# Two products of an up projection change places in a written order of work

## The chip, the cores and the metric

The kernel runs on one core of one Trainium2 chip. What counts is the time on the device, in microseconds (us), as the median of several executions. The engines are named as in the profile: PE is TensorE (its matmuls; PEld its weight loads), DVE is VectorE, ACT is ScalarE, POOL is GpSimd, and SP is SyncE, which here only issues DMAs. Each engine has a queue of its own and works through it in order; an instruction that has to wait for another engine holds up all that stands behind it on its own.

## The reference

One layer of a hybrid decoder on 1024 tokens with 1024 features, in float32:

```
h = x + W_o [ RMSNorm(attention(u)) ; RMSNorm(ShortConv(u)) ],   u = RMSNorm(x) @ W_in
a = rms_norm(h) @ w_up;  gate, up = split(a)            # 2 x 2816 features
gate = causal_dwconv(gate, ffn_conv_w) + ffn_conv_b     # three taps along the tokens
h = h + (silu(gate) * up) @ w_down
h = h + sigmoid(rms_norm(h) @ w_pg) * (p @ w_pe)
```

The change lies in the second line, the up projection, at its very beginning.

## The kernel before

Float32 products are made of halves: a number is split in a high half, rounded to the form that PE takes (`fp32r`), and a low half, the rest. A product of two such numbers is three matmuls (high by high, high by low, low by high). ACT casts the high half, and DVE subtracts it from the number to get the low half.

**The up projection.** The 2816 features are 22 blocks `f` of 128. For a block, gate and up by two halves of the tokens by two halves of the 1024 inputs make a 2 by 2 block product, which the kernel forms with seven products in place of eight (Strassen's scheme in Winograd's form). Product `(f, i)` is 12 matmuls of 128x512: four chunks `k` of the inputs by three halves. The table `PRODUCT` says for each `i` which combination of the activations it takes, in which PSUM accumulator it adds up, and which combination of the weights it takes:

```
    PRODUCT = {1: ("b11", "x", "a11"), 2: ("b21", "x", "a12"), 3: ("b22", "z", "s4"), 4: ("t4", "y", "a22"),
               5: ("t1", "z", "s1"), 6: ("t2", "y", "s2"), 7: ("t3", "y", "s3")}
```

So `(1, 2)`, the second product of block 1, takes the activations `b21` and the raw weights `a12` and adds onto `ux` of block 1, where `(1, 1)` has been. Behind `(f, 1)` stands a copy of `ux` to SBUF by ACT (tile `uv`, line 1084), and it has to be made before `(f, 2)` adds to the same accumulator. `(0, 5)` takes the activations `t1` (tiles `formt1` with the chunk's number) and the sum of weights `s1` = `a21` + `a22`, and it is the first to write `uz` of block 0; behind it DVE makes `uw` from `uz` and `uv` (line 1052), and only then may `(0, 3)` add onto `uz`.

**Weights.** `fetch` loads a raw quarter of a block's weights (tile `wup`, 256 KB, a DMA of SP's queue, line 91) and POOL adds or subtracts quarters to the sums (tile `wsum`, line 1010): for a block `s1`, `s2` = `s1` - `a11`, `s4`, `s3`. `split` then casts the high half on ACT (`wbh`, line 1023) and subtracts the low half on DVE (`wbl`, line 1024), four places of the order ahead of the product. `ahead` fetches, and thereby puts in the order of SP and POOL, seven to nine places ahead.

**Activations.** In the same written order, ahead of and between the first products, stand four pairs `("A", k)`: the output projection of rows `k` and `k + 4` for the second half of the tokens (PSUM tiles `bp`), and in between eight small products `("E", m)` (tiles `be`, copied by ACT to `emb` and stored to `eD`). A pair is followed by a chain: DVE scales `bp` (line 882) and adds the residual to get `hm` (line 884), ACT multiplies by a gain to get `y` (line 890), DVE makes the combinations `yt` (line 904), ACT casts their high halves and DVE subtracts the low halves (both into `form`, lines 909 and 913). The chain of pair `k` gives chunk `k` of `t1`, `t2`, `t3`, `t4` and `b22`; the last chunk, `formt13` and its like, comes from `("A", 3)`.

**What sets the order.** All of this lies in a `manual_schedule`: the instructions stand on each engine as the loop over `order` emits them. Where tiles lie in SBUF is settled when the program is built (`auto_bufs=True`): tiles share places, and a tile that takes over a place waits for the last reader of the tile that was there.

Of the kernel before, what the change touches and what calls it, by code (L numbers as in the profile page):

```python
# [48 lines left out]
def _emit(nc, tc, d, out, tap=lambda *a: None):  # L49
# [909 lines left out]
    for m in range(KC):  # L959
# [4 lines left out]
        if m == 3:  # L964
# [23 lines left out]
           "s4": (OP.subtract, "a12", "s2")}  # L988
    AHEAD = 4
    order = [("A", 0), ("E", 0), ("E", 1), ("E", 2), ("A", 1), ("E", 3), ("E", 4), ("E", 5), ("A", 2), ("E", 6), ("E", 7),  # L990
             (0, 1), ("A", 3), (1, 1), (0, 2), (1, 2),
             (0, 5), (0, 6), (0, 3), (0, 7), (1, 5), (0, 4), (1, 6), (1, 3), (1, 7)]
    for f in range(2, NF):
        order += [(f, 1), (f - 1, 4), (f, 6), (f, 5), (f, 2), (f, 7), (f, 3)]
    order.append((NF - 1, 4))
# [364 lines left out]
def _build(arrays, tap=None):  # L1360
    nc = _bacc.Bacc("TRN2", target_bir_lowering=False, num_devices=1)
    d = {k: nc.dram_tensor("in_" + k, v.shape, _mybir.dt.from_np(v.dtype), kind="ExternalInput").ap()
         for k, v in arrays.items()}
    out = nc.dram_tensor("out_0", (KC, P, T), F32, kind="ExternalOutput").ap()
    with _tile.TileContext(nc, auto_bufs=True) as tc:  # L1365
        _emit(nc, tc, d, out, *([lambda n, a: tap(nc, n, a)] if tap else []))
    return nc
# [8 lines left out]
```

## Time and profile before

| | us |
|---|---|
| median of 3 executions | 1471.7 |
| lowest and highest of the 3 | 1469.31 and 1472.52 |
| the profiled execution, its own time | 1464.96 |
| its span, first to last instruction | 1463.1 |

The 1.9 us between span and own time lie around the instructions. Durations below come from the profiled execution, which was 6.7 us faster than the median of the timed ones; the profile's times count from the start of its span. The first block of the up projection begins at 667 us, and the whole projection ends at about 1113 us.

### The profile page before, as it was taken

The page shows a single profiled execution, that of the slowest core. Times are in us where ns is not written, and L with a number is a line of the kernel's source. Part 1 is how long each engine was busy: PE and PEld are TensorE (multiplying, and loading weights), DVE is VectorE, ACT ScalarE, POOL GpSimd, SP SyncE. Part 2 cuts the span into 40 slices and gives each one's busy share as a digit, 9 for nine tenths or more (in the row PEclk, how much of TensorE's full clock was granted, in tenths as well). Part 3 has the DMA queues.
Part 4 walks back from the last instruction along what each step waited for, and adds up shares of the span by engine and source line. Part 5 has one row for each costly group of instructions (what it writes and reads, how often), then busy time and mean ns, then how long its engine had stood idle before and what let it go on. Part 6 is the DMA issues. An engine that isn't in the chain of part 4 may idle for free.

```text
span 1463.1 us, 19683 instructions
## 1 busy us (share of the span) xinstructions
PE 1423.8 (97%) x7223; PEld 1161.9 (79%) x7223; DVE 990.0 (68%) x1612; ACT 605.1 (41%) x1240; POOL 477.5 (33%) x462
## 2 busy tenths in 40 slices
PE   7999999999999999998999999999999999999998
PEld 5787898997777777786788888888788887888787
DVE  7645467555788888788767887777786464377443
ACT  4110132136788898775423333333334322045311
POOL 3221242366445558202432334332330424002200
PEclk9999999999999999999999999999999999999999
DMA  7221214300000002274022212222216432241132
GB/s 263 75 73 45 88 39 150 133 1 1 1 1 1 1 1 87 75 260 148 29 86 87 69 61 87 87 87 86 86 52 219 160 139 88 75 169 44 53 99 80
DMA packets 52945, 123.91 MB, mean 85 GB/s; under 512 B 6001, under 2 KB 8945, under 8 KB 52849
## 3 DMA queue, kind: packets, MB, share of 16 engines
q1 hardware_dynamic: 52848, 122.65, 24.7%
q8 instruction: 57, 0.93, 0.3%
q14 instruction: 40, 0.32, 0.1%
HBM read 94.32 MB, written 28.31 MB: 84 GB/s over the span
## 4 chain that ended last, share of the span: by engine, by line
PE 50%; DVE 2%; issue 1%; ACT 0%; POOLq 0%; POOL 0%; ACTq 0%; DVEq 0%
PE uy L1044 12%; PE uz L1044 8%; PE ux L1044 8%; PE ba L103 6%; PE ba L102 6%; PE ba L101 6%; PE bd L103 1%; PE bd L102 1%; PE bd L101 1%; DVE wbl L1024 0%; DVE actl L1181 0%; DVE yt L904 0%; PE ba L165 0%; POOLq L1365 0%; DVE ua L1071 0%
## 5 line engine op out<-in xcount | busy, mean ns | idle before, releaser
L1044 PE MATMUL uy<-formt,wbh 128*128 128x512 f32 x528 | 165.2, 394 | 0.7 <-ACT wbh L1023 0.3
L694 POOL TENSOR_SCALAR P<-P,sc,consts 128x64 f32<-128x64 f32 (+8 forms) x192 | 130.4, 689 | 98.4 <-DVE sc L692 93.8
L1010 POOL TENSOR_TENSOR wsum<-wup,wup 128x512 f32<-128x512 f32 x44 | 74.8, 1700 | 266.4 <-DMA wup<-in_w_up 205.4
L677 DVE TENSOR_REDUCE nmax<-b 128x1 f32<-128x64 f32 (+8 forms) x192 | 96.9, 540 | 35.3 <-PE b L669 34.5
L1024 DVE TENSOR_TENSOR wbl<-wsum,wbh 128x512 fp32r<-128x512 f32 x88 | 77.1, 877 | 63.1 <-ACT wbh L1023 63.1
L1044 PEld LDWEIGHTS uy<-formt,wbh 128*128 128x128 f32 x528 | 99.0, 188 | 24.9 <-issue 1.2
L683 ACT ACTIVATE P<-b,nmax 128x64 f32<-128x64 f32 (+8 forms) x192 | 108.9, 576 | 18.9 <-DVE nmax L677 7.7
L1044 PE MATMUL ux<-formb,wbh 128*128 128x512 f32 x352 | 111.6, 398 | 5.1 <-ACT uv L1084 5.1
L102 PE MATMUL ba<-actl,wh 128*128 128x512 f32 x288 | 113.3, 394 | 1.9 <-DVE actl L1181 1.9
L103 PE MATMUL ba<-acth,wl 128*128 128x512 f32 x288 | 112.9, 393 | 0.0
L101 PE MATMUL ba<-acth,wh 128*128 128x512 f32 x288 | 112.1, 392 | 0.0
L143 DVE TENSOR_TENSOR wl<-wraw,wh 128x1024 fp32r<-128x1024 f32 (+3 forms) x85 | 89.2, 1052 | 23.2 <-POOL wh L142 10.8
L1044 PE MATMUL uy<-formt,wbl 128*128 128x512 f32 x264 | 104.4, 395 | 0.0
L719 PE MATMUL ba<-consts,P 128*128 128x128 f32 x592 | 90.2, 276 | 5.0 <-DVE pl L735 2.5
L1198 DVE TENSOR_TENSOR h<-h,ba 128x512 f32<-128x512 f32 x64 | 43.9, 686 | 71.8 <-PE ba L103 71.5
L142 POOL TENSOR_SCALAR wh<-wraw 128x1024 fp32r<-128x1024 f32 (+2 forms) x37 | 48.2, 1307 | 130.0 <-PE b L102 48.1
L719 PEld LDWEIGHTS ba<-consts,P 128*128 128x128 f32 x592 | 68.3, 142 | 23.7 <-issue 7.1
L1071 DVE SCALAR_TENSOR_TENSOR ua<-ug,consts,ua 128x1023 f32<-128x1023 f32 (+1 forms) x44 | 85.1, 1933 | 0.0
L735 DVE TENSOR_TENSOR pl<-ba,ph 128x512 fp32r<-128x512 f32 x120 | 78.8, 679 | 7.5 <-ACT ph L731 6.3
L1044 PEld LDWEIGHTS ux<-formb,wbh 128*128 128x128 f32 x352 | 67.0, 191 | 21.1 <-ACT uv L1084 5.5
L1100 ACT ACTIVATE ua<-ua 128x1024 f32<-128x1024 f32 x22 | 23.3, 1061 | 144.4 <-DVE ua L1071 144.4
L140 ACT CAST wh<-wraw 128x512 fp32r<-128x512 f32 (+2 forms) x48 | 30.3, 654 | 115.0 <-PE ba L102 102.5
(321 smaller groups left out, 3944.8 us busy)
## 6 DMA issues: line engine op xcount, KB each, us to landing
wup<-in_w_up SPq DMA_DIRECT2D x88, 256.0 KB, 4.1
aD<-ua SPq DMA_DIRECT2D x22, 512.0 KB, 2.9
t<-aD SPq DMA_DIRECT2D x22, 512.0 KB, 4.9
wraw<-in_w_down SPq DMA_DIRECT2D x32, 256.0 KB, 5.3
wraw<-in_wA SPq DMA_DIRECT2D x13, 512.0 KB, 3.6
hinc<-in_xT SPq DMA_DIRECT2D x16, 256.0 KB, 3.3
h<-t SPq DMA_DIRECT2D x16, 256.0 KB, 2.3
hin<-h SPq DMA_DIRECT2D x16, 256.0 KB, 4.5
```

The costliest lines, as they stand in the source:

```text
L101: pe.matmul(ps, ah, bh, start=first, stop=False)
L102: pe.matmul(ps, ah, bl, start=False, stop=False)
L103: pe.matmul(ps, al, bh, start=False, stop=last)
L143: dve.tensor_sub(lo, raw, f32(hi))
L677: dve.tensor_reduce(nmax[:, b:b + 1], ps[:, o:o + w], axis=AX.X, op=OP.max, negate=True)
L683: act.activation(pr[:, pc:pc + w], ps[:, o:o + w], AF.Exp, bias=nmax[:, b:b + 1], accum_out=den[:, b:b + 1])
L694: pool.tensor_scalar(pr[:, pc:pc + w], pr[:, pc:pc + w], sc[:, b:b + 1], gates[:, t, hd * 3 + b:hd * 3 + b + 1], op0=OP.mult, op1=OP.mult)
L719: pe.transpose(pt[0:k, r * P:(r + 1) * P], probs[u, r][:, pc:pc + k], ident)
L735: dve.tensor_sub(pl, pt[0:k], f32(ph))
L1024: dve.tensor_sub(lo, y, f32(hi))
L1044: pe.matmul(ps, a[:, k], b, start=new and k == n_mm == 0, stop=k == 3 and n_mm == 2, skip_group_check=not new)
L1071: dve.scalar_tensor_tensor(a[:, j:], y[:, 0:T - j], cw[:, 2 - j:3 - j], a[:, j:], op0=OP.mult, op1=OP.add)
```

## The change

`(0, 5)` stood right behind `(1, 2)` and now stands right ahead of it:

```diff
     order = [("A", 0), ("E", 0), ("E", 1), ("E", 2), ("A", 1), ("E", 3), ("E", 4), ("E", 5), ("A", 2), ("E", 6), ("E", 7),
-             (0, 1), ("A", 3), (1, 1), (0, 2), (1, 2),
-             (0, 5), (0, 6), (0, 3), (0, 7), (1, 5), (0, 4), (1, 6), (1, 3), (1, 7)]
+             (0, 1), ("A", 3), (1, 1), (0, 2), (0, 5), (1, 2),
+             (0, 6), (0, 3), (0, 7), (1, 5), (0, 4), (1, 6), (1, 3), (1, 7)]
```

Everything that hangs on a place of the order moves along: the 12 matmuls, the two splits, the loads and sums, and what follows a product (`uw` behind `(0, 5)`, the gate `ug` behind `(1, 2)`). The build also lays 664 tiles at other places in SBUF, so that some waits are other ones.

On PE, after the products `(0, 1)`, `("A", 3)`, `(1, 1)`, before the change (the first row is the end of `(0, 2)`; `ux_1669` belongs to block 1, `wbh_1647` are the weights `a12` of block 1, `wbh_1667` those of `s1` of block 0; in brackets what a row waits for):

```order
L1044 MATMUL ux_1642_7556<-formb213_1524_7088,wbl_1641_7553 128x512
L1044 MATMUL ux_1669_7654<-formb210_1503_7001,wbh_1647_7576 128x512 [waits Activation_49]
L1044 MATMUL ux_1669_7654<-formb210_1503_7001,wbh_1647_7576 128x512
L1044 MATMUL ux_1669_7654<-formb210_1503_7001,wbl_1648_7577 128x512 [waits DVE_49]
L1044 MATMUL ux_1669_7654<-formb211_1509_7028,wbh_1647_7576 128x512 x2
```

And in the changed kernel (`wbh_1647` now holds `s1` of block 0, `wbh_1667` now `a12` of block 1):

```order
L1044 MATMUL ux_1642_7556<-formb213_1524_7088,wbl_1641_7553 128x512
L1044 MATMUL uz_1680_7702<-formt10_1554_7208,wbh_1647_7576 128x512 x2
L1044 MATMUL uz_1680_7702<-formt10_1554_7208,wbl_1648_7577 128x512 [waits DVE_49]
L1044 MATMUL uz_1680_7702<-formt11_1590_7351,wbh_1647_7576 128x512 x2
L1044 MATMUL uz_1680_7702<-formt11_1590_7351,wbl_1648_7577 128x512
L1044 MATMUL uz_1680_7702<-formt12_1626_7496,wbh_1647_7576 128x512 x2
L1044 MATMUL uz_1680_7702<-formt12_1626_7496,wbl_1648_7577 128x512
L1044 MATMUL uz_1680_7702<-formt13_1664_7640,wbh_1647_7576 128x512 [waits Activation_49]
L1044 MATMUL uz_1680_7702<-formt13_1664_7640,wbh_1647_7576 128x512 [waits DVE_49]
L1044 MATMUL uz_1680_7702<-formt13_1664_7640,wbl_1648_7577 128x512
L1044 MATMUL ux_1669_7654<-formb210_1503_7001,wbh_1667_7650 128x512 [waits Activation_49]
L1044 MATMUL ux_1669_7654<-formb210_1503_7001,wbh_1667_7650 128x512
```

The matmul that waits for ACT's copy `uv` of block 1 now has twelve others ahead of it; ten of these need nothing of the last chunk's low half, and the eleventh does.

On SP's queue, some 30 us earlier, the loads of the same weights (before, 1601 is `a12` of block 1, 1606 and 1607 are `a21` and `a22` of block 0; after, 1601 and 1602 are `a21` and `a22`, and 1607 is `a12`):

```order
 L1128 DMA eD_3_7119<-emb_1598_7386 128x512
 L91 DMA wup_1601_7403<-in_w_up 128x512
-L1128 DMA eD_4_7120<-emb_1602_7405 128x512
-L1128 DMA eD_4_7120<-emb_1603_7408 128x512
-L91 DMA wup_1606_7425<-in_w_up 128x512
+L91 DMA wup_1602_7405<-in_w_up 128x512
+L1128 DMA eD_4_7120<-emb_1603_7407 128x512
+L1128 DMA eD_4_7120<-emb_1604_7410 128x512
 L91 DMA wup_1607_7427<-in_w_up 128x512
```

The two quarters that POOL's first sum needs go out one and two places of weights earlier, ahead of the stores `eD_4`.

On ACT, in the chain of pair 2 (`y2`, `y6` are its two rows, `hm_1615` is the sum of the second), before:

```order
L890 ACTIVATE y2_0_1619_7482<-hm_1614_7466,consts_1_61 128x512 [waits DVE_49]
L890 ACTIVATE y6_0_1620_7484<-hm_1615_7470,consts_1_61 128x512 [waits DVE_49,Activation_49,Pool_49]
L909 CAST formb222_1621_7486<-y6_0_1620_7484 128x512 [waits DMAHW1_49,Activation_49]
L894 ACTIVATE t2_1622_7488<-hm_1614_7466 128x512 [waits DMAHW3_49]
L894 ACTIVATE t2_1623_7490<-hm_1615_7470 128x512 [waits DVE_49]
```

After:

```order
L890 ACTIVATE y2_0_1619_7482<-hm_1614_7466,consts_1_61 128x512 [waits DVE_49]
L890 ACTIVATE y6_0_1620_7484<-hm_1615_7470,consts_1_61 128x512 [waits DVE_49,Activation_49]
L909 CAST formb222_1621_7486<-y6_0_1620_7484 128x512 [waits DMAHW2_49,Activation_49]
L894 ACTIVATE t2_1622_7488<-hm_1614_7466 128x512 [waits DMAHW5_49]
L894 ACTIVATE t2_1623_7490<-hm_1615_7470 128x512 [waits DVE_49]
```

And on DVE one step ahead in the same chain, after the change (before it, the third row had no `Pool_49` among its waits):

```order
L884 TENSOR_TENSOR hm_1614_7466<-bp_1612_7439,hin_1542_7157 128x512 [waits DMAHW5_49,DMAHW3_49,DVE_49]
L882 TENSOR_TENSOR bp_1613_7440<-bp_1613_7440,rab_440_3041 128x512 [waits PE_49]
L884 TENSOR_TENSOR hm_1615_7470<-bp_1613_7440,hin_1543_7159 128x512 [waits DMAHW0_49,DVE_49,Pool_49]
L913 TENSOR_TENSOR formt31_1616_7473<-yt_1589_7349,formt31_1616_7473 128x512 [waits DMAHW6_49,DMAHW5_49,Activation_49]
L913 TENSOR_TENSOR formt21_1617_7475<-yt_1591_7354,formt21_1617_7475 128x512 [waits Activation_49]
```

A wait for POOL has gone from ACT's `y6` to DVE's `hm`. By the semaphore's count it is the same one in both programs, for POOL's fourth sum (`s3` of block 0, the last reader of `a11` and `a21`): before, `y6` takes over the place of `a11`; after, `hm` takes over that of `a21`.

## Rows read from the trace of the kernel before

**Rows 1.** The page: busy time and share of the span by engine.

```profile
span 1463.1 us, 19683 instructions
...
PE 1423.8 (97%) x7223; PEld 1161.9 (79%) x7223; DVE 990.0 (68%) x1612; ACT 605.1 (41%) x1240; POOL 477.5 (33%) x462
```

**Rows 2.** Busy time by engine in one stretch: from:to, length, PE (count), PEld, DVE, ACT, POOL; PEclk, DMA.

```profile
725.00:1110.00 385.00, 384.80 (x1656) 310.70 (x1655) 296.19 (x357) 127.04 (x194) 127.39 (x73) 1.00 0.24 82
```

**Rows 3.** Who waited for whom, PE, whole span: us in total, times, longest.

```profile
PE ux L1044 <- ACT uv L1084: 5.1, 1, 5.1
...
PE uz L1044 <- DVE uw L1052: 0.9, 1, 0.9
```

**Rows 4.** Timeline of PE: start, length, instruction, [idle before it, releaser].

```profile
680.94 0.40 PE L1044 MATMUL ux<-formb,wbl 128*128 128x512 f32 x1
686.45 1.22 PE L1044 MATMUL ux<-formb,wbh 128*128 128x512 f32 x2 [5.11 <-ACT uv L1084]
...
690.73 0.62 PE L1044 MATMUL uz<-formt,wbh 128*128 128x512 f32 x2
...
693.52 0.63 PE L1044 MATMUL uy<-formt,wbh 128*128 128x512 f32 x2
...
698.19 0.70 PE L1044 MATMUL uz<-formb,wbh 128*128 128x512 f32 x2 [0.94 <-DVE uw L1052]
```

**Rows 5.** Stretches with their granted clock, as rows 2, and PE's timeline there.

```profile
687.00:690.00 3.00, 3.00 (x9) 2.38 (x8) 3.00 (x6) 1.48 (x3) 0.00 (x0) 0.58 0.27 90
...
1242.00:1245.00 3.00, 2.44 (x11) 2.04 (x12) 2.92 (x5) 0.00 (x0) 0.00 (x0) 1.00 0.61 180
...
1242.56 0.50 PE L102 MATMUL ba<-actl,wh 128*128 128x512 f32 x1 [1.88 <-DVE actl L1181]
```

**Rows 6.** Timeline of ACT.

```profile
667.41 0.72 ACT L890 ACTIVATE y<-hm,consts 128x512 f32<-128x512 f32 x1 [6.07 <-POOL wsum L1010]
...
684.78 0.62 ACT L909 CAST formt<-yt 128x512 fp32r<-128x512 f32 x1 [0.15 <-DVE yt L904]
...
685.82 0.58 ACT L1084 COPY uv<-ux 128x512 f32<-128x512 f32 x1
```

**Rows 7.** Timeline of POOL.

```profile
661.30 1.29 POOL L1010 TENSOR_TENSOR wsum<-wup,wup 128x512 f32<-128x512 f32 x1 [17.44 <-DMA wup<-in_w_up]
...
665.63 1.74 POOL L1010 TENSOR_TENSOR wsum<-wup,wup 128x512 f32<-128x512 f32 x1
678.02 1.32 POOL L1010 TENSOR_TENSOR wsum<-wup,wup 128x512 f32<-128x512 f32 x1 [10.65 <-DMA wup<-in_w_up]
680.62 1.60 POOL L1010 TENSOR_TENSOR wsum<-wsum,wup 128x512 f32<-128x512 f32 x1 [1.28 <-DVE formt L913]
```

**Rows 8.** Timeline of DVE; a row with x2 or x3 merges that many.

```profile
662.69 0.69 DVE L884 TENSOR_TENSOR hm<-bp,hin 128x512 f32<-128x512 f32 x1
663.30 4.62 DVE L913 TENSOR_TENSOR formt<-yt,formt 128x512 fp32r<-128x512 f32 x3
667.84 1.28 DVE L904 TENSOR_TENSOR yt<-y,y 128x512 f32<-128x512 f32 x2
...
677.50 2.99 DVE L913 TENSOR_TENSOR formt<-yt,formt 128x512 fp32r<-128x512 f32 x3
680.41 2.36 DVE L904 TENSOR_TENSOR yt<-y,y 128x512 f32<-128x512 f32 x2
...
684.62 0.68 DVE L913 TENSOR_TENSOR formt<-yt,formt 128x512 fp32r<-128x512 f32 x1
...
686.55 0.69 DVE L1024 TENSOR_TENSOR wbl<-wsum,wbh 128x512 fp32r<-128x512 f32 x1
```

**Rows 9.** Timeline of SP's queue, the issue of the loads named in the change.

```profile
653.95 0.40 SPq L91 DMA_DIRECT2D wup<-in_w_up  x1
...
655.56 0.99 SPq L91 DMA_DIRECT2D wup<-in_w_up  x2
```

**Rows 10.** The tile `wup`: its 88 loads from issue to landing.

```profile
DMA to landing us min/median/max: 2.6/4.1/6.4
```

## The prediction

> **What bounds the kernel now.** I read the page first: PE is busy for 97% of the span, 1423.8 of 1463.1 us, and no other engine comes near [rows 1]. So the time is PE's, and a change of order that adds and removes no work can only move what PE waits. The stretch in which the up projection repeats itself has nothing to give: 384.80 of 385.00 us busy at a clock of 1.00 [rows 2]. I then read the list of waits for PE alone. Two of its rows lie where the change lies: 5.1 us, once, for ACT's copy `uv`, and 0.9 us, once, for DVE's `uw` [rows 3]. PE's timeline shows the first as 5.11 us ahead of `(1, 2)`, whose first row starts at 686.45, and the second as 0.94 us ahead of `(0, 3)` at 698.19 [rows 4]. The wait has a tail: `(1, 2)` runs from 686.45 to 690.73, 4.28 us, where the twelve matmuls of the next product take 2.79 (690.73 to 693.52) [rows 4]. The clock says why: 0.58 of full speed was granted from 687 to 690 [rows 5], so most of these matmuls ran at 1.2 in place of 2.4 GHz after the engine had stood still. That is 1.49 us more.
>
> Why is `uv` late? It ends at 686.40, as third in a row of ACT instructions without a gap behind a cast `formt` that starts at 684.78 and waited for DVE's `yt` [rows 6]. DVE is the late one, and it has no gap from 663 on [rows 8]. Followed back, the chain of pair 2 had begun late: ACT's `y` stood for 6.07 us and started at 667.41, released by POOL's fourth weight sum [rows 6], and POOL had started its first at 661.30 after 17.44 us of waiting for a load [rows 7].
>
> **DVE under POOL.** Three subtractions `formt` from 663.30 take 4.62 us while POOL adds [rows 7, 8]; the two `yt` that follow, with POOL idle, take 1.28, so 0.64 each, and three would take 1.9 [rows 8]. The same happens twice more in the chain that ends at `uv`: three `formt` from 677.50 take 2.99 (1.1 too much, beside the sum at 678.02) and two `yt` from 680.41 take 2.36 (1.1 too much, beside the sum at 680.62) [rows 7, 8]. But `hm` at 662.69, which reads PSUM, takes its 0.69 under a sum [rows 8]. The Trainium skill ("SBUF — State Buffer", section "SBUF: two separate sides") has it that DVE instructions with two SBUF inputs and GpSimd instructions hold one pair of ports by an exclusive lock, the loser waiting for the whole of the other. The rows agree as far as they go: the two-input forms grow, the one that reads PSUM doesn't. By the page alone a step that merely moves POOL's sums would gain nothing, since each has to collide with some other subtraction; that would bring the sum below to the second case.
>
> **The change, part by part.**
>
> 1. *The ten matmuls.* `(0, 2)` issues its last at 680.94, so PE is free at 681.17 (0.23 a matmul: 2.79 over 12). `(0, 5)` comes next in place of the wait. Ten of its twelve need nothing of the last chunk's low half: they end at 683.5. The eleventh needs the subtraction that ran from 684.62 to 685.30 [rows 8].
>
> 2. *The loads and POOL.* Before, the loads that POOL waited for were issued as a pair from 655.56 on [rows 9], the second from about 656.1, and POOL began 5.2 us after that [rows 7]. Now they are the one issued at 653.95 and the next behind it [rows 9], about 654.45. Bounds: no earlier landing at all (661.30), or the same 5.2 us (659.65). I take 659.65, because nothing in the queue ahead of them has changed. DVE at that time works on PSUM or waits, so four sums run at the first one's 1.29 and a small step between, 1.36 in all, 5.4: the fourth ends at 665.1, against 667.37 before (665.63 + 1.74) [rows 7].
>
> 3. *The wait that moved.* The fourth sum now releases `hm` on DVE, where it released `y` on ACT. `hm` slips from 662.69 to about 665.1, and the three subtractions queued behind it slip along. They now run with POOL done: 665.75 + 1.9, so `yt` starts at about 667.6, where it started at 667.84 [rows 8]. A gain of 0.25, and `y` itself is ready at 666.6, before it is wanted.
>
> 4. *The later sums.* The sum at 680.62 was released by a `formt` of DVE [rows 7]. In the changed build it takes over another place and, by the semaphore's count, waits for the low half `wbl` of `(0, 6)`, which comes behind `uv` in the chain. Its 1.1 us of collision leave the chain. The sum at 678.02 waits for loads as before, issued about 1 us earlier since ACT's copies ahead of their stores come earlier; what it costs DVE lies between 0 and 1.1 less than before, and I take 0.5. In all the chain is 0.25 + 0.5 + 1.1 = 1.85 us earlier when it reaches `formt13`.
>
> 5. *What PE then waits.* The low half of the last chunk is there at 685.30 - 1.85 = 683.45, just when the eleventh matmul wants it. `(0, 5)` ends at 683.95. `uv` ends at 686.40 - 1.85 = 684.55, which costs `(1, 2)` a wait of 0.6. Its low half `wbl` is where that of `(0, 5)` stood, at 686.55 to 687.24 [rows 8], less 1.85: 685.4, and the third matmul, due at 685.0, waits 0.4. `(1, 2)` ends at 684.55 + 2.79 + 0.4 = 687.75, where `(0, 5)` ended at 693.52: 5.8 us earlier. With two waits of half a microsecond I keep the clock up: after an idle 1.88 us elsewhere the granted clock stayed at 1.00 [rows 5].
>
> 6. *`uw`.* It stood behind DVE's step of the norm, which waits for PE; now it stands where the gate `ug` of block 1 was, ahead of that step, and is done before `(0, 3)` is due. The 0.94 us [rows 4] go. `ug` slips behind, and is wanted some 20 us later. The spread of the norm and ACT's `rfb` hang on PE and move with it.
>
> Sum against the profiled execution: 5.11 + 1.49 + 0.94 = 7.54 us of waiting and slow clock, less 1.0 that remains, is 6.5 us: own time 1464.96 to 1458.5. Behind that lies the full stretch of rows 2, which only starts earlier. The timed runs lie 6.7 us above the profiled one and nothing says that the part differs there, so 1471.7 - 6.5 = 1465.2.
>
> **The rivals.**
>
> *Only the product fills the gap, DVE is no faster.* Loads land when they did, or the collisions come back at other subtractions. Then the eleventh matmul waits from 683.5 to 685.35, `(0, 5)` ends at 685.8, `(1, 2)` starts at 686.45 as before, waits 0.35 for its low half and ends at 689.6: 3.9 earlier, plus 0.94, is 4.85. If the clock falls after these two idle pieces, `(1, 2)` pays 1.49 again and 3.4 remain. 1466.9 to 1468.3. For it: the sums have to be made somewhere. Against it: one collision moves behind `uv` by its own wait. The lock of the Trainium skill (page and section as above) speaks for this rival, wherever a moved sum finds another subtraction.
>
> *The change doesn't do what it says.* The gain of the product is eaten at the next waits: `(0, 6)` and `(0, 3)` hang on the same DVE queue, and if the whole queue comes 2 us later than in the case just told, 1.4 to 2.8 are left, which a measurement cannot tell from nothing: about 0.2%, 2.9 us, is the limit here. 1469 to 1471.7. Against it: behind the subtraction at 686.55 [rows 8] stand three more and then the one that `(0, 6)` needs, 0.6 each, done by 689.7 in the old timing and 687.85 in the new one, and the third matmul of `(0, 6)` is due at 688.2.
>
> *Slower: DVE stands at `hm`.* The new wait blocks all of DVE, where the old one blocked ACT. If the loads land later than at 659.65, everything behind `hm` slips by as much, up to `uv`. 6.5 us of gain and 1.5 for the slow clock leave 5.0: from a landing at 664.7 on, 10 us after the issue, the kernel is slower, and with a landing at 668, 3.3 slower, 1475. Against it: the slowest of 88 such loads takes 6.4 us [rows 10]. A wait of 0.35 us in each of the 20 repeated blocks, by the new places of the tiles, would weigh the same; there POOL has 127 of 385 us of work, ACT 127, DVE 296 [rows 2], which leaves room.
>
> **How the numbers follow.** My forecast has 0.62, the filled gap alone 0.22, no visible change 0.11, slower 0.05. The likeliest gives 1465.2. All of the 7.54 gone would be 1464.2, and the three runs shown differ by 3.2 us among themselves, so the low end is 1463.0. The high end takes in the whole of the second case and a little spread, 1468.9. What is left out holds 0.16 above it and a little below. Faster by over 0.2% is 0.62 + 0.22, less a little for a filled gap that measures small, plus a part of the third case: 0.84. Within 0.2% it is 0.11, slower 0.05.
>
> **What would show it.** In the changed profile PE's row for `uv` should fall from 5.1 to about 0.6 us or name another releaser, and the row for `uw` should be gone. POOL's first sum should start at about 659.7 and its fourth end near 665; ACT's `y` should follow `hm` at once, with DVE idle some 2.5 us ahead of `hm`. The two `yt` near 680 should take 1.3 in place of 2.4, with POOL's second sum of block 1 at about 687. The clock should stay at 1.00 from 684 to 690. PE's full stretch should keep its 385 us. I am wrong if POOL starts no earlier, if the clock falls all the same, if a new wait shows in the repeated blocks, or if the down projection, in which the scheduler now puts one cast of ACT ahead of a copy, gains a gap of its own.

## The result and the profile after

The changed kernel takes 1462.0 us (median of 6 executions, 1458.2 to 1462.9), the kernel before, timed beside it, 1471.2 (6 executions, 1468.4 to 1475.8). The ratio is 0.9931, with a 95% interval of 0.9911 to 0.9951: 10.2 us faster, between 7.2 and 13.1. Timed again with other kernels, the ratio was 0.9935 (0.9915 to 0.9956). 1465.2 was predicted, with a range from 1463.0. The direction is right and the gain is too small: 6.5 us in place of some 10.

The profiled execution of the changed kernel has a span of 1460.3 us, only 2.8 less than that of before. The page, beside [rows 1]:

```profile
span 1460.3 us, 19666 instructions
...
PE 1427.2 (98%) x7223; PEld 1164.7 (80%) x7223; DVE 986.6 (68%) x1612; ACT 605.4 (41%) x1240; POOL 475.4 (33%) x462
```

PE is busy 3.4 us longer, with the same matmuls. So two spans tell little here, and the reading has to go by places. In PE's list of waits the row of `uv` is gone, where [rows 3] have 5.1. The row of `uw` has 0.2 us, and PE's timeline puts these at 928.94, in a repeated block, and not at `(0, 3)`, where the 0.9 of [rows 3] were:

```profile
PE uz L1044 <- DVE uw L1052: 0.2, 1, 0.2
```

```profile
928.94 0.70 PE L1044 MATMUL uz<-formb,wbh 128*128 128x512 f32 x2 [0.20 <-DVE uw L1052]
```

PE's timeline shows the place. The second row is the start of `(0, 5)`, the fourth that of `(1, 2)`, then come `(0, 6)` and `(0, 3)`:

```profile
685.68 0.62 PE L1044 MATMUL ux<-formb,wbh 128*128 128x512 f32 x2
...
686.37 0.62 PE L1044 MATMUL uz<-formt,wbh 128*128 128x512 f32 x2
...
688.43 0.63 PE L1044 MATMUL uz<-formt,wbh 128*128 128x512 f32 x2
...
689.12 0.69 PE L1044 MATMUL ux<-formb,wbh 128*128 128x512 f32 x2
...
690.29 0.62 PE L1044 MATMUL ux<-formb,wbh 128*128 128x512 f32 x2
...
692.39 0.63 PE L1044 MATMUL uy<-formt,wbh 128*128 128x512 f32 x2
...
696.00 0.71 PE L1044 MATMUL uz<-formb,wbh 128*128 128x512 f32 x2
```

`(0, 2)` ends at 686.37, 5.2 us later than before (681.17), and `(0, 3)` starts at 696.00. **The stretch from the one to the other took 17.0 us before [rows 4] and takes 9.6 now: 7.4 us less.** `(0, 5)` runs without a wait, and `(0, 3)` starts without one. `(1, 2)` loses 0.5 us behind its first two rows, which take 1.17 in place of 0.70, and nothing else.

The same place in windows of time, the up projection's repeated part (as [rows 2], put 2.19 earlier as `(0, 3)` is), and a stretch far ahead of the change; the columns are as in [rows 2]:

```profile
722.81:1107.81 385.00, 384.67 (x1656) 310.43 (x1655) 296.74 (x357) 128.02 (x195) 127.17 (x73) 1.00 0.24 82
684.00:687.00 3.00, 3.00 (x14) 2.46 (x14) 2.96 (x6) 2.81 (x6) 0.00 (x0) 1.00 0.80 212
687.00:690.00 3.00, 2.85 (x13) 1.86 (x12) 2.96 (x6) 2.88 (x6) 0.00 (x0) 1.00 0.39 143
410.00:420.00 10.00, 9.27 (x34) 7.48 (x35) 4.73 (x10) 3.05 (x9) 1.74 (x4) 0.50 0.00 0
```

The last row is where most of the span's gain is hidden. In the profile of before it reads:

```profile
410.00:420.00 10.00, 8.89 (x60) 7.03 (x60) 7.55 (x17) 6.37 (x16) 3.90 (x6) 1.00 0.00 0
```

The granted clock was 0.50 after and 1.00 before, 34 matmul rows against 60, behind the same idle 2.46 us of PE in attention, before and after:

```profile
410.95 0.63 PE L719 MATMUL ba<-consts,P 128*128 128x128 f32 x4 [2.46 <-DVE pl L735]
```

```profile
410.73 1.09 PE L719 MATMUL ba<-consts,P 128*128 128x128 f32 x4 [2.46 <-DVE pl L735]
```

The matmuls that PE does from 405 to 420 in the profile of before take 15.0 us there and 19.3 after, by the starts of their rows. The place lies ahead of the change, and a later profile of the kernel before has the same ten microseconds of half clock there, so it is not put down to the change; but it hides 4.3 us of the gain in this pair of profiles. What is called one stretch of half clock below lasts as long as the shortest here, 3.4 us by the trace's clock records; where the clock stays low two or three times as long, it counts as two or three stretches.

The chain, beside [rows 6 to 8]; 5.2 us are to be taken off each time. ACT, where `y` now waits for `hm` and no longer for POOL, and `uv`:

```profile
670.05 0.72 ACT L890 ACTIVATE y<-hm,consts 128x512 f32<-128x512 f32 x1 [3.47 <-DVE hm L884]
...
688.45 0.58 ACT L1084 COPY uv<-ux 128x512 f32<-128x512 f32 x1
```

SP, the issue of the two loads that POOL's first sum needs:

```profile
659.34 0.88 SPq L91 DMA_DIRECT2D wup<-in_w_up  x2
```

POOL, its first and fourth sum and the two of block 1:

```profile
663.92 1.30 POOL L1010 TENSOR_TENSOR wsum<-wup,wup 128x512 f32<-128x512 f32 x1 [14.76 <-DMA eD<-emb]
...
667.94 1.29 POOL L1010 TENSOR_TENSOR wsum<-wup,wup 128x512 f32<-128x512 f32 x1
680.67 1.28 POOL L1010 TENSOR_TENSOR wsum<-wup,wup 128x512 f32<-128x512 f32 x1 [11.44 <-DMA wup<-in_w_up]
692.44 1.62 POOL L1010 TENSOR_TENSOR wsum<-wsum,wup 128x512 f32<-128x512 f32 x1 [10.49 <-issue]
```

DVE:

```profile
669.26 0.69 DVE L884 TENSOR_TENSOR hm<-bp,hin 128x512 f32<-128x512 f32 x1 [1.37 <-POOL wsum L1010]
669.87 1.89 DVE L913 TENSOR_TENSOR formt<-yt,formt 128x512 fp32r<-128x512 f32 x3
671.67 1.29 DVE L904 TENSOR_TENSOR yt<-y,y 128x512 f32<-128x512 f32 x2
...
682.34 1.89 DVE L913 TENSOR_TENSOR formt<-yt,formt 128x512 fp32r<-128x512 f32 x3
684.15 1.29 DVE L904 TENSOR_TENSOR yt<-y,y 128x512 f32<-128x512 f32 x2
...
687.28 0.68 DVE L913 TENSOR_TENSOR formt<-yt,formt 128x512 fp32r<-128x512 f32 x1
...
689.21 0.69 DVE L1024 TENSOR_TENSOR wbl<-wup,wbh 128x512 fp32r<-128x512 f32 x1
...
693.43 1.18 DVE L1024 TENSOR_TENSOR wbl<-wsum,wbh 128x512 fp32r<-128x512 f32 x1
```

All three groups of DVE's steps that POOL had stretched now take their short time: 1.89 for 4.62, 1.89 for 2.99, 1.29 for 2.36. POOL's sum at 680.67 lies beside DVE's steps on PSUM. The one at 692.44 is behind the whole chain; it meets the `wbl` at 693.43, which takes 0.5 us longer than the others, but no matmul up to `(0, 3)` waited for that.

### The profile page after: what moved, and what is told of

It reads as the page before. It is cut to its first block, busy times and chain, and to the rows that moved or that the text cites. A ratio compares the mean times of both kernels' runs of the same rounds, so it can differ in the third digit from the quotient of the medians.

```text
span 1460.3 us, 19666 instructions
## 1 busy us (share of the span) xinstructions
PE 1427.2 (98%) x7223; PEld 1164.7 (80%) x7223; DVE 986.6 (68%) x1612; ACT 605.4 (41%) x1240; POOL 475.4 (33%) x462
## 4 chain that ended last, share of the span: by engine, by line
PE 40%; DVE 6%; issue 3%; DMA 1%; ACT 1%; POOL 0%; POOLq 0%; ACTq 0%; DVEq 0%; SPq 0%
PE uy L1044 8%; PE ba L103 6%; PE ba L102 6%; PE ba L101 6%; PE uz L1044 5%; PE ux L1044 5%; DVE ua L1071 2%; DVE wbl L1024 2%; DMA aD<-ua 1%; PE bd L103 1%; PE bd L102 1%; PE bd L101 1%; DVE uc L1052 1%; DVE ua L1075 1%; ACT wbh L1023 1%
```

## The experiments

Two questions were open. What is each half of the change worth? And why do the timed executions of before lie 3.5 to 10.8 us above its profiled one? Theory A: they lose more at the place of the change. Theory B: they lose it elsewhere, where a stretch of half clock comes and goes.

**The kernel before once more.**

> The kernel before once more, to find why its timed executions lie 4 to 11 us above the one that was profiled. Theory A (at the place of the change): the wait of 5.1 us for uv and the slow clock behind it are longer in most executions than in the profiled one; a second profile shows more than 5.1 us of wait or more than 3.4 us of half clock near 686, and the rest is as it was. Theory B (elsewhere): the stretch from the end of (0, 2) to the start of (0, 3) takes 17.0 us again, and another stretch of half clock shows somewhere else, such as behind the idle 2.46 us at 408, where the profile of the changed kernel has one of 10 us that cost it 4.2 us; spans then go with the mean clock, about 1463 at 0.996 and 1467 at 0.994. By either theory the time is that of the kernel before, 1468 to 1476.

Ratio 1.0001 (0.9985 to 1.0017), 1471.8 us. The profile had a wait for `uv` of 4.97, one stretch of half clock behind it, and others near 58, 356 and 417. Of 30 executions of before in this comparison the fastest took 1465.3 us at a mean clock of 0.996, the slowest 1476.0 at 0.990. Over all 30, (1 - mean clock) times span, which is the time that the clock took away, rises together with the execution's time, about 1 us for 1 us. So most of the scatter is clock, and part of it elsewhere: B, as far as one profile goes.

**Products and splits moved, loads and sums as before.** The changed kernel, but `ahead` follows a list `prep` in which the two products stand as before (its first line is shown without the `order.append` that it follows):

```diff
+    prep = list(order); p, q = prep.index((1, 2)), prep.index((0, 5)); prep[p], prep[q] = prep[q], prep[p]
-            if j < len(order) and order[j][0] not in ("A", "E"):
-                f, i = order[j]
+            if j < len(order) and prep[j][0] not in ("A", "E"):
+                f, i = prep[j]
```

> The changed kernel, but the loads and POOL's sums stay in the order of before: products and splits alone have moved. By the steps of the prediction the chain of the last chunk is then about 1.85 us later than in the changed kernel, PE waits for uv or for the low half again, and the stretch from the end of (0, 2) to the start of (0, 3), 17.0 us before and 9.6 in the changed kernel, takes 17.0 - 4.85 = 12.2; 2.6 us slower than the changed kernel, 1464.6. The rival (the ten matmuls do it all, the earlier sums are worth nothing) has 9.6 in the stretch and no difference to the changed kernel, 1462.

1463.8 us, ratio 0.9939 (0.9918 to 0.9961). The interval holds both times that were expected, so the time alone does not tell them apart, nor this kernel from the changed one; the trace does. PE waits twice again, at the eleventh matmul of `(0, 5)` and for `uv`:

```profile
687.06 0.50 PE L1044 MATMUL uz<-formt,wbh 128*128 128x512 f32 x1 [1.43 <-DVE formt L913]
...
688.12 0.73 PE L1044 MATMUL ux<-formb,wbh 128*128 128x512 f32 x2 [0.33 <-ACT uv L1084]
```

and DVE's three subtractions meet both sums of block 1, which POOL makes at 679.64 (1.38 us) and 681.10 (1.63):

```profile
679.18 4.09 DVE L913 TENSOR_TENSOR formt<-yt,formt 128x512 fp32r<-128x512 f32 x3
683.20 1.28 DVE L904 TENSOR_TENSOR yt<-y,y 128x512 f32<-128x512 f32 x2
```

2.2 us too much, 1.1 for each sum. The stretch from `(0, 2)` to `(0, 3)` takes 11.9 us: the product and its splits are worth 5.2 of the 7.4 us, the earlier sums 2.2.

**Loads and sums moved, products and splits as before.** The same edit the other way round.

> The kernel before, but the loads and POOL's sums go in the order of the changed kernel; products and splits stand as before. By the steps of the prediction hm waits for POOL in place of y, the subtractions near 680 lose their company, and the wait for uv falls from 5.1 to about 3.2 us; by what the profile after shows (both collisions gone) to 2.7; the clock falls all the same. That is 1.9 to 2.4 us faster than before. If the earlier sums are worth nothing, the wait stays 5.1 us.

1468.0 us, ratio 0.9973 (0.9955 to 0.9992). PE and DVE:

```profile
691.58 1.22 PE L1044 MATMUL ux<-formb,wbh 128*128 128x512 f32 x2 [3.18 <-ACT uv L1084]
```

```profile
684.21 2.48 DVE L913 TENSOR_TENSOR formt<-yt,formt 128x512 fp32r<-128x512 f32 x3
```

The wait falls by 1.9 us, as the steps have it, and the clock still falls. Here POOL's sum started at 683.64, released by DVE, and cost the three subtractions 0.6 us; in the changed kernel it was released by its load, and cost nothing. So the same order of sums can meet the subtractions or miss them. The Trainium skill ("SBUF — State Buffer", section "SBUF: two separate sides") tells of ports that DVE's forms with two SBUF inputs and GpSimd lock against each other. The rows agree: each whole sum beside such steps costs DVE some 1.1 us. They don't bear out what the prediction drew from it, that a sum that is moved has to meet some other subtraction and that nothing is gained: in the changed kernel the sum at 680.67 and the four ahead of it meet none, and the one at 692.44 meets a `wbl` for 0.5 us, where no matmul up to `(0, 3)` waits for it.

**Idle time filled, nothing moved.** In `product`, ahead of `(1, 2)` (written out here over several lines; the two lines that let `(0, 5)` take this accumulator and clear it are left out):

```diff
+        if (f, i) == (1, 2):
+            up[0]["z"] = PS("uz", 2)
+            for k in range(12):
+                pe.matmul(up[0]["z"], wh[:, k % 4], form["b21"][k % 4][0], start=k == 0, stop=k == 11)
```

> The kernel before with twelve more matmuls of no use ahead of (1, 2), on PE alone; they add into the accumulator that (0, 5) clears afterwards. They fill 2.8 us of the wait for uv, so 2.3 us of idle remain, and (1, 2) can start no earlier. If the fall of the clock comes from the length of the idle time, (1, 2) takes 2.8 in place of 4.28 us and the gain is 1.5 us against the profiled execution, 1469.7. By theory A (the slow clock at this place is what the timed executions of before lose more of) the time falls by up to 6 us, 1465 to 1467; by theory B by 1.5. If the clock falls all the same, nothing is gained.

1466.1 us, ratio 0.996 (0.9945 to 0.9975): 5.9 us faster (3.7 to 8.1), though what it adds is useless and `(1, 2)` still starts 5.1 us behind the end of `(0, 2)` (5.3 before). PE's timeline and a window:

```profile
680.80 2.88 PE L1040 MATMUL uz<-formb,wbh 128*128 128x512 f32 x12
685.94 0.73 PE L1044 MATMUL ux<-formb,wbh 128*128 128x512 f32 x2 [2.25 <-ACT uv L1084]
```

```profile
686.00:689.00 3.00, 3.00 (x13) 2.49 (x14) 3.00 (x6) 1.97 (x4) 0.00 (x0) 1.00 0.25 90
```

Behind an idle 2.25 us the clock stays at 1.00, where it fell to 0.50 behind 4.97 and 3.18. The stretch from `(0, 2)` to `(0, 3)` takes 15.5 us, 1.5 less than in the first profile of before. 5.9 is more than that; theory A has to be looked at again. The gain is nearly all clock: over these 12 executions (1 - mean clock) times span is 6.7 us in mean, over the 30 of before 11.6. Where on the way the part beyond 1.5 us was saved, the one profile doesn't show.

**The idle near 409 filled**, in the changed kernel and in that of before, with twelve matmuls behind the second of the four matmuls that sum the squares of the first tile of tokens (line 817; they add to columns that nobody reads; written out over several lines):

```diff
             pe.matmul(ps[:, 0:1], sq[:, c], ones[:, 0:1], start=c == 0, stop=c == 3)
+            if len(sums) == 1 and c == 1:
+                for _ in range(12):
+                    pe.matmul(ps[:, 128:512], identr, ksl[:, 0:384], start=False, stop=False)
```

> The changed kernel with twelve matmuls of no use in the idle 2.46 us of PE near 409 (they add into columns that nobody reads). In the six profiles so far that idle was followed by 0, 3, 1, 0, 3 and 1 stretches of half clock of 3.4 us each; in mean 1.3, and each costs 1.7 us. If the idle causes them, they go, and the kernel is 2.3 us faster than the changed one, 1459.5; mean clock up by 0.0015. If something else sets the clock there, nothing changes, 1461 to 1462.

> The kernel before with the same twelve matmuls near 409, none at the place of the change. If the timed executions of before lose their surplus near 409, this kernel is 3 to 5 us faster than before and only 7 to 8 us slower than the changed kernel with the same filling, which is what the stretch from the end of (0, 2) to the start of (0, 3) is worth by the profiles (7.4). If the surplus lies at the place of the change or behind it, it is 2.3 us faster than before, and 10 us slower than the other. Its profile also shows once more how long the clock is low behind the wait for uv: 3.4 us as in two profiles of before, or more.

> The changed kernel once more, beside the two with the filling: 1461 to 1462, 0.69% less than before. In the profile 9.6 us from the end of (0, 2) to the start of (0, 3), no half clock between 684 and 690 of the old time scale, and half clock at some of the places 56, 352, 409, 1241 and 1376, as in the other profiles.

The changed kernel alone took 1461.5 us (0.9935), with the filling 1457.6 (0.9908, 0.9886 to 0.9929); before with the filling 1468.4 (0.9982, 0.9969 to 0.9996) against 1472.2. By the medians the filling is worth 3.9 us in the one and 3.8 in the other (by its interval 0.6 to 4.6 in before; in the changed kernel the intervals with and without it overlap), and between the two filled kernels lie 10.8. The expectation had either a small gap between the filled kernels or a small gain of the filling; the gain was the larger one and so was the gap. A gain that is the same in both kernels can't make their difference, so the surplus of before does not lie near 409. PE's filling, and the window 405 to 420 with it:

```profile
408.00 2.34 PE L817 MATMUL ba<-ksl 128*128 128x384 f32 x12
```

```profile
405.00:420.00 15.00, 14.84 (x99) 12.10 (x99) 11.50 (x28) 11.82 (x31) 6.64 (x8) 1.00 0.00 0
```

The second profile of the changed kernel, without filling, has 0.89 there, and 9.6 us again from `(0, 2)` to `(0, 3)`. That of before with the filling shows two stretches of half clock, not one, behind the wait for `uv`.

**The idle near 1368 and 1376 filled too**, with three and six matmuls ahead of the two spreads (written out):

```diff
                     rp = rstd(pssq[:, s], 4, D, "rp", 2)
+                    pd = psb()
+                    for _ in range(6 if c else 3):
+                        pe.matmul(pd, wh[:, 0], eh[c // 512][0], start=True, stop=True)
                     spread_all(rp, 4, rpb[:, s], psb)
```

> As the changed kernel with the filling near 409, and further matmuls of no use in the idle 0.77 and 1.69 us ahead of the last two spreads, near 1368 and 1376, where five of six profiles show one stretch of half clock behind the second. If the idle causes it: 1.4 us (1.7 times 5/6) faster than with the filling near 409 alone, 1458, and 13 to 14 us faster than before. If the filling itself comes late there and holds up the spread, or the clock falls all the same: no gain or a loss of up to 1 us.

> The kernel before with the fillings near 409, 1368 and 1376, so that the wait for uv is the only long idle time left behind 360. If the surplus of before lies in the half clock behind that wait, this kernel stays 10 to 11 us slower than the changed kernel with the same fillings (mean 1457.9), 1468 to 1469, and its profile shows one to three stretches of half clock near 686 and none behind it. If the surplus came from the places near 409 or 1376, it is 1465 or less, 7.4 us slower.

The changed kernel so filled took 1457.5 us (0.9905, 0.9884 to 0.9927): the 1.4 us that were expected beyond the filling near 409 don't show. Before so filled took 1467.7 (0.9963, 0.9949 to 0.9977). By the two ratios they lie 8.5 us apart, by the medians 10.2. 1465 or less, as it should be if the surplus lay near 409 or 1376, is not reached; but 8.5 with these intervals can't be told from the 7.4 of that case, so this speaks against 1376 and doesn't rule it out. Its profile has one stretch of half clock behind `uv`, and one near 1244, which was not expected.

**Three more profiles of the kernel before.**

> The kernel before, one profiled execution, to count the stretches of half clock behind the wait for uv. So far 1, 1 and 2 in three profiles in which that wait is about 5 us. A stretch costs 1.7 us; the changed kernel has none there. The idle time that the change takes away is 5.7 us, so the 9 to 11 us that are measured want 2 to 3 stretches in mean. If these three looks show one each, the surplus is not at this place.

> As the look before: 2 to 3 stretches of half clock in mean behind the wait for uv if the surplus lies there, one if not.

> As the two looks before: 2 to 3 stretches of half clock in mean behind the wait for uv if the surplus lies there, one if not.

Each shows two stretches. The first of them, in PE's timeline (the last row is the start of `(0, 5)`) and in a window, beside the 0.58 that [rows 5] have in the window of the same length:

```profile
691.82 1.22 PE L1044 MATMUL ux<-formb,wbh 128*128 128x512 f32 x2 [4.77 <-ACT uv L1084]
...
695.82 1.05 PE L1044 MATMUL ux<-formb,wbh 128*128 128x512 f32 x2
...
697.10 0.76 PE L1044 MATMUL uz<-formt,wbh 128*128 128x512 f32 x2
```

```profile
693.00:696.00 3.00, 3.00 (x9) 2.32 (x8) 3.00 (x6) 0.85 (x2) 0.00 (x0) 0.50 0.40 128
```

All of `(1, 2)` runs at half clock, 5.28 us in place of 2.79; in [rows 4] it took 4.28. And the second of them shows, in PE's waits from 712 to 1118, what [rows 2] had not:

```profile
PE uz L1044 <- DVE uw L1052: 1.5, 3, 0.9
PE uy L1044 <- ACT wbh L1023: 0.3, 1, 0.3
```

## Why the prediction was right in its mechanism and too small in its sum

What the two kernels take by places, worked out from the starts of PE's rows in five profiles of before (the first, the copy and the last three) and two of the changed kernel:

| us | before, lowest to highest | mean | changed | difference of means |
|---|---|---|---|---|
| start to the end of `(0, 2)` | 681.2 to 688.9 | 685.7 | 682.8, 686.4 | 1.1 |
| from there to the start of `(0, 3)` | 16.8 to 18.0 | 17.5 | 9.6, 9.6 | 7.9 |
| `(0, 3)` to the end of the projection | 413.9 to 416.0 | 415.0 | 413.5, 414.1 | 1.2 |
| the idle near 1241 and what follows | 11.2 to 12.8 | 11.8 | 11.2, 11.2 | 0.6 |
| start of PE's last matmul to the end of the span | 5.0, all five | 5.0 | 4.7, 4.7 | 0.3 |

Every other stretch is the same within about 0.1. The first line is ahead of the change and mostly clock: chance.

1. *The ten matmuls*: right, and more than that, since the last two did not wait either.

2. *The loads and POOL*: right in kind, outside its bounds by 0.9. The first sum started at 658.7 on the old scale (659.65 was forecast, and at the latest 661.30), some 4.1 us behind the issue of the second load (about 659.8 in the profile after) in place of 5.2. The row names a store of `eD` as the last thing that released it. The fourth sum ended at 664.0 (665.1).

3. *The wait that moved*: as told; `hm` is released by POOL, with 1.4 us of idle DVE ahead of it and not 2.5, and `y` follows at once. `yt` starts at 666.5 in place of 667.6. Little of this lasts: in the next pair DVE waits for PE, and the subtractions there start only 0.36 us earlier than before.

4. *The later sums*: **the first term that was mis-sized.** For the sum at 678.02 a gain of 0.5 was taken, out of 0 to 1.1; it was the whole 1.1, because the load released it early enough to lie beside work on PSUM. The sum behind it left the chain, as forecast (687.2, against "about 687"). The chain comes 0.36 + 1.1 + 1.07 = 2.5 us earlier, not 1.85. The experiments show that with the products alone moved DVE still meets the collisions (4.09 us for three), and that the sums alone bring the wait down by 1.9 us.

5. *What PE then waits*: 1.0 us was forecast and 0.5 remained: no wait for `uv`, and half a microsecond for the low half of `(1, 2)`. The clock stayed at 1.00, as said.

6. *`uw`*: right, and whole: `(0, 3)` starts without a wait.

In all the two profiles show 7.4 us at this place, where the sum had 6.5. Of the 0.9 us between, 0.5 is the wait that did not remain (steps 4 and 5). 0.3 is a matter of reading: the sum took the idle times that the rows give, 5.11 and 0.94, while by the starts of the rows the two gaps cost 5.28 (681.17 to 686.45) and 1.07 (1.89 us from the eight small matmuls to `(0, 3)`, now 0.82).

**The step that failed is the last one**, the carrying over: "The timed runs lie 6.7 us above the profiled one and nothing says that the part differs there". It does differ there. The profiled execution of before had one stretch of half clock behind the wait for `uv`; the five profiles have 1, 1, 2, 2 and 2, and those with two take 17.8 to 18.0 us at this place in place of 16.8 to 17.0 (with the idle near 409 filled, two came with 17.2, so the price of a second is not fixed). So the 1.49 us for the slow clock were sized from a lesser case. And it is the only one of the five without waits of PE for `uw` in the repeated blocks: the other four have 1.3, 1.2, 1.5 and 0.5 us of them, the two profiles of the changed kernel 0.2 and 0.5. "Behind that lies the full stretch of rows 2, which only starts earlier" holds for that one execution.

The lines of the table at and behind the change add up to 10.0 us, within the measured 7.2 to 13.1. Against the sum of 6.5 that is 3.5 more: 0.9 at the place in the first pair of profiles, 0.5 by the second stretch, 1.2 in the blocks, 0.6 near 1241 and 0.3 behind the last matmul, in means over few profiles. The timed executions say the same of the clock: (1 - mean clock) times span is 11.7 us in mean over 17 executions of before, and 8.0 and 8.8 over the two sets of six executions of the changed kernel. By this estimate 2.9 to 3.6 us of the difference are clock, not 1.49; it is an upper one, since half clock costs nothing while PE stands idle or has done its last matmul.

The 1.2 us in the blocks are measured, but they are not shown to come from the order of the products: the kernel before with its idle time filled, where nothing moved, has no wait for `uw` there either, and with the idle near 409 filled it has 0.5. What makes them is open, and so is whether the difference near 1241 (a stretch of half clock there in two of five profiles of before, in none of the changed one) is more than chance, and where the last 0.3 come from. Both theories held a part, as far as these profiles go: A for what the change gains, B for most of the scatter of the executions.

The rivals: the filled gap alone, without the earlier sums, is the second experiment; it is real, and the place is worth 5.2 us that way (4.85 was worked out), but both came together. The slower case did not come: the loads landed sooner than assumed, not later. The repeated blocks kept 384.67 of 385 us, no new wait of PE above 0.5 us came up behind the change, and the down projection shows no gap of its own.

## What to carry to other kernels

A stall of PE can cost more than its length: price the clock behind it as well, and price it from several profiles, since one execution may show the lesser case. When a wait ahead of a product is long, another product that is ready belongs in front of it, and its splits and sums have to move along, or part of the gain (here 2.2 of 7.4 us) waits at the next operand. Where matmuls stand idle for some microseconds and nothing useful is ready, useless ones can be worth their place: twelve of them gave 3.9 us here by the medians, and with them the changed kernel ran at 1457.6 us, faster than either kernel without.

## What the runs showed of the hardware

The same idle near 409, 2.46 us (1.69 in one profile), was followed by a clock of 1.00 in two of the ten profiles without filling (the first of before among them), and by a stretch of half clock, of up to the ten microseconds shown above, in the other eight; with the idle filled, in none of four. Behind idle times of 4.76 to 5.11 us the clock fell in all seven profiles that had them, behind 3.18 in the one, behind 2.25 and 1.43 in none. Near 352 it fell after waits of only 0.89 and 0.79 us in 10 of 14 profiles. A DVE subtraction with both inputs in SBUF takes 0.63 us by itself, and a POOL sum that lies wholly beside such steps adds 1.1 us to DVE's row; `hm`, which reads PSUM, kept its 0.69.
